# A two-layer hybrid encoder: wide products with weights stationary and 256 tokens streamed, residual stream kept by channels

## The chip, the cores and the metric

The kernel runs on one core of one Trainium2 chip. The metric is the device time of one execution in microseconds (us). A core has a matrix engine (PE, with PEld its weight loads), a vector engine (DVE), a scalar engine (ACT), a general engine (POOL) and a queue engine (SP) that here issues nearly all DMAs. Each engine takes its instructions in a fixed order and waits on semaphores for the others.

A matrix product holds one operand of 128x128 in the array (the stationary one, brought in by a load) and streams the other past it, column by column. Both operands have the contraction on their partitions; the result goes to PSUM with the stationary operand's columns on its partitions.

## The reference

```python
for i in range(DEPTH):                       # 2 layers, x is 256 tokens x 1024 channels, float32
    h = rms_norm(x, ffn1_norm[i])
    x = x + 0.5 * swiglu_ffn(h, ffn1_w_gate[i], ffn1_w_up[i], ffn1_w_down[i])   # 1024 -> 2816 -> 1024
    h = rms_norm(x, mix_norm[i])
    (s5_u, gla_q, gla_k, gla_v, gla_g, gla_zf, gla_zb, at_q, at_k, at_v) = split(h @ w_in[i])
    y_s5, y_gla, y_attn = s5_branch(...), gla_branch(...), attn_branch(...)     # each 256 x 512
    gates = sigmoid(h @ w_merge_gate[i] + b_merge_gate[i])                      # 3 x 1024 columns
    merged = sum(gates[b] * (y[b] @ w_branch[b]) for b in range(3))
    x = x + merged @ w_out[i]
    h = rms_norm(x, ffn2_norm[i])
    x = x + 0.5 * swiglu_ffn(h, ffn2_w_gate[i], ffn2_w_up[i], ffn2_w_down[i])
return rms_norm(x, final_norm)
```

## The kernel before

**Wide products.** Every large product is made of three products of float32r operands: `load` brings a weight tile (two 128-row k tiles by 512 columns) by DMA, ACT rounds it to `hi` (L209) and DVE makes the rest `lo` (L210); activations are split the same way (`hTh`/`hTl`, `sTh`/`sTl`, `mTh`/`mTl`, the branches' `y..h`/`y..l`). `mm3` (L219 to L221) then does hi.hi, hi.lo and lo.hi. The stationary operand is a 128x128 tile of activations, channels on partitions, 128 tokens as columns; 512 columns of weights are streamed, so the result has tokens on partitions. There are two token tiles (`NT` = 2).

**Where transposes come from.** The residual `x` is held with tokens on partitions. `norm` transposes it on PE (L263, four 128x128 transposes into one PSUM tile `pt`, four such tiles), multiplies by the gain (L265), splits it (L267, L268), and gets the sum of squares from ACT's accumulator (L272); the root `rstd` goes into the evacuations as one number per partition. In `ffn`, `evac` takes a block of 256 gate and 256 up columns: ACT does silu from PSUM (L294), DVE the product (L295), PE transposes the result twice (L298), ACT and DVE split it (L300, L301). GLA's q and k are transposed in `ev_tr` (L714), the gated sum in `merge` (L1127).

**One product in the other form.** `s5_glu` (L887 to L889) has weights stationary already and streams 256 tokens: `hi[:, ms]` is the stationary operand and `yh[:, k]` the moving one.

**Order.** `stream` goes over blocks of 512 columns in chunks of four k tiles; its first two blocks take their chunks in turn (`lead=2`). `weave` emits a main part and, after each of its steps, some steps of side parts: the S5 tables of a layer (`s5_tables`) beside the FFNs ahead of the mixer, the three branches inside the mixer. A scheduler then sets each engine's order from what was emitted. The tables end, for each quarter, in products `kp` on PE (L603), copies `ks` (L606, L607, L610), POOL copies `kx` (L627) and eight DMAs to DRAM (L630).

Of the kernel before, what the change touches and what calls it, by code (L numbers as in the profile page):

```python
# [15 lines left out]
P = 128  # L16
D = 1024
# [21 lines left out]
# main steps before a side part begins, and its steps per main step  # L39
# [12 lines left out]
# columns of the constants: those for the mixer, then those for the tables  # L52
# [4 lines left out]
def constants():  # L57
    """Arrays that depend on shapes alone, one row per partition."""
# [24 lines left out]
def cols(*parts):  # L83
    """Columns of weights [K, N] side by side: for the k tiles [a, z)."""
    def f(a, z):
        res, o = [], 0
        for w, cs in parts:
            res.append((w[a * P:z * P, cs].rearrange("(k p) n -> p k n", p=P), 0, o))
            o += cs.stop - cs.start
        return res  # L90
    return f


def weave(main, sides, up=nullcontext):
    """Emit main; from its step `start` on, `per` steps of a side part after each step of main.
    sides: list of [start, per, generator]. Whatever is left of them comes in the end."""
# [14 lines left out]
def rest(*gens):  # L111
    """Emit what is left of these parts, in turn, as one step."""
# [13 lines left out]
class Enc:  # L126
    def __init__(self, tc, ctx, ins, out):
# [15 lines left out]
        self.x = c.tile([P, NT, D], F32, name="x")  # L143
        self.cst = c.tile([P, C_MIX], F32, name="cst")
        self.row = {}
        with tc.high_priority():
            self.vectors("ffn1_norm", eng=nc.scalar)
            for h in range(2):
                for t in range(NT):
                    hs = slice(h * 512, (h + 1) * 512)  # L150
                    nc.scalar.dma_start(self.x[:, t, hs], ins["x"][0, t * P:(t + 1) * P, hs])
# [13 lines left out]
    def vectors(self, *names, eng=None):  # L165
        """Parameters of channels, to partitions: [128 channels, (layer, tile)]"""
        nc = self.nc
        eng = eng or nc.sync
        n = 48 if len(names) > 1 else 16
# [3 lines left out]
        for name in names:  # L173
# [6 lines left out]
            else:  # L180
                eng.dma_start(vec[r:r + DEPTH * KD], self.ins[name].rearrange("l (k p) -> (l k) p", p=P))
                self.row[name] = (vt, r, KD)
# [10 lines left out]
    def load(self, pieces):  # L193
        """pieces: list of (dram AP [partitions, k tiles, columns], first partition, first column)"""
# [21 lines left out]
    def mm3(self, ps, act, w, first, last):  # L216
        """act: (hi, lo) [128 k, 128 tok]; w: (hi, lo) [128 k, n]"""
# [4 lines left out]

    def stream(self, act, nk, blocks, lead=1):
        """act(k, t) -> (hi, lo). blocks: list of (pieces(k0, k1) in k tiles, width, evac(t, ps)).
        The first `lead` blocks take their first chunks together."""
# [3 lines left out]
        ps = {}  # L229
        for b, c in order:  # L230
            pieces, width, evac = blocks[b]
            k0, k1 = chunks[c]
            w = self.load(pieces(k0, k1))
            for t in range(NT):
# [6 lines left out]
            for s in range(0, k1 - k0, SUB):  # L241
                for t in range(NT):
                    for k in range(k0 + s, min(k1, k0 + s + SUB)):
                        self.mm3(ps[b, t][:, :width], act(k, t), w[k - k0], k == 0, k == nk - 1)
            if c == len(chunks) - 1:
                for t in range(NT):
                    evac(t, ps[b, t][:, :width])
            yield

# [1 line left out]
    def norm(self, name, l):  # L251
# [3 lines left out]
        sq = self.st.tile([P, 2, NT], F32, name=f"sq{self.n}", tag="sq")  # L255
# [3 lines left out]
        for c in range(2):  # L259
            for t in range(NT):  # L260
                pt = self.ptr.tile([P, 4, P], F32, name=self.nm("pt"), tag="tr")
# [915 lines left out]
```

## Time and profile before

| | |
|---|---|
| median of three runs | 1378.12 us (1378.01 to 1379.51) |
| profiled execution, span | 1376.2 us |
| PE busy | 1336.0 us, 97% |
| PE weight loads busy | 1061.6 us, 77% |
| DVE busy | 1018.4 us, 74% |
| ACT busy | 698.6 us, 51% |
| DMA queue of the weights, share of 16 engines | 57.5% |
| granted TensorE clock, mean | 0.996 |

The span is that of one profiled execution, from its first to its last instruction; 1.9 us lie between it and the median. Busy times of matrix products overlap, because products are pipelined: the pitch from start to start is what counts, and it is read from the timeline.

### The profile page before, as it was taken

How to read it: one execution, taken by the hardware profiler on the slowest of the kernel's cores; microseconds unless marked ns; L12 is line 12 of the kernel's file. 1: busy time of each engine (PE TensorE's matmuls, PEld its weight loads, DVE VectorE, ACT ScalarE, POOL GpSimd, SP SyncE). 2: the span in 40 equal slices, each digit the busy share in tenths (PEclk: the TensorE clock that was granted, in tenths of full speed). 3: DMA queues.
4: the chain of work that ended last, by engine and by line, in shares of the span. 5: the costliest groups of instructions: out<-in, count | busy, mean ns of one | idle time of the engine just before them, and what ended most of it. 6: DMA issues, size and time to landing. Idle time of an engine off the chain costs nothing.

```text
span 1376.2 us, 19506 instructions
## 1 busy us (share of the span) xinstructions
PE 1336.0 (97%) x6920; PEld 1061.6 (77%) x6920; DVE 1018.4 (74%) x1826; ACT 698.6 (51%) x1102; POOL 73.5 (5%) x104
## 2 busy tenths in 40 slices
PE   7999999999999999999999999999999999999997
PEld 5878788778787678768877777887787877888886
DVE  5899975779986789996465775457799767655553
ACT  5545345447585355445355454354475754555542
POOL 1020210000100000110000000000001000000000
PEclk9999999999999999999999999999999999999999
DMA  7766666565453366666665646566654533655662
GB/s 227 195 211 224 234 222 179 189 205 198 140 183 122 107 161 206 200 202 221 198 195 173 204 149 204 180 178 202 196 200 134 168 107 122 191 178 186 182 213 76
DMA packets 201201, 249.88 MB, mean 182 GB/s; under 512 B 40856, under 2 KB 134600, under 8 KB 201104
## 3 DMA queue, kind: packets, MB, share of 16 engines
q1 hardware_dynamic: 200496, 247.59, 57.5%
q8 instruction: 54, 0.88, 0.3%
q10 hardware_dynamic: 608, 1.06, 0.2%
q14 instruction: 43, 0.35, 0.1%
HBM read 234.44 MB, written 13.11 MB: 180 GB/s over the span
## 4 chain that ended last, share of the span: by engine, by line
PE 63%; issue 17%; DVE 13%; DMA 3%; ACT 3%; POOL 1%; SPq 0%; POOLq 0%; ACTq 0%; DVEq 0%
PE mm L220 18%; PE mm L219 17%; PE mm L221 17%; DVE lo L210 4%; PE S L818 1%; DMA raw<-in_ffn_w_gate 1%; DMA raw<-in_ffn_w_up 1%; PE as L1070 1%; ACT hi L209 1%; PE ao L1092 1%; DVE t L349 1%; PE st L298 1%; DVE run L836 1%; DVE run L835 1%; PE apt L1085 1%
## 5 line engine op out<-in xcount | busy, mean ns | idle before, releaser
L210 DVE TENSOR_TENSOR lo<-raw,hi 128x1024 fp32r<-128x1024 f32 x412 | 499.4, 1217 | 191.7 <-ACT hi L209 184.1
L209 ACT CAST hi<-raw 128x1024 fp32r<-128x1024 f32 x412 | 427.7, 1042 | 305.6 <-PE mm L221 276.3
L220 PE MATMUL mm<-lo,hTh 128*128 128x512 f32 (+1 forms) x1120 | 445.3, 398 | 5.3 <-DVE lo L210 4.9
L219 PE MATMUL mm<-hi,hTh 128*128 128x512 f32 (+1 forms) x1120 | 437.6, 396 | 2.7 <-ACT hTh L267 2.7
L221 PE MATMUL mm<-hi,hTl 128*128 128x512 f32 (+1 forms) x1120 | 436.1, 392 | 0.0
L220 PEld LDWEIGHTS mm<-lo,hTh 128*128 128x128 f32 x1120 | 211.2, 189 | 51.7 <-DVE lo L210 9.2
L219 PEld LDWEIGHTS mm<-hi,hTh 128*128 128x128 f32 x1120 | 211.2, 189 | 45.5 <-ACT hTh L267 3.8
L221 PEld LDWEIGHTS mm<-hi,hTl 128*128 128x128 f32 x1120 | 210.6, 188 | 40.6 <-DVE hTl L268 0.3
L220 PE MATMUL mm<-lo,sThffn 128*128 128x512 f32 x352 | 138.9, 395 | 2.0 <-DVE lo L210 2.0
L221 PE MATMUL mm<-hi,sTlffn 128*128 128x512 f32 x352 | 138.1, 393 | 0.0
L219 PE MATMUL mm<-hi,sThffn 128*128 128x512 f32 x352 | 136.4, 395 | 0.0
L300 ACT CAST sThffn<-st 128x256 fp32r<-128x256 f32 x88 | 32.6, 372 | 128.7 <-PE st L298 128.5
L220 PEld LDWEIGHTS mm<-lo,sThffn 128*128 128x128 f32 x352 | 66.4, 189 | 16.6 <-DVE lo L210 2.5
L221 PEld LDWEIGHTS mm<-hi,sTlffn 128*128 128x128 f32 x352 | 66.5, 189 | 14.1
L219 PEld LDWEIGHTS mm<-hi,sThffn 128*128 128x128 f32 x352 | 66.5, 189 | 13.8
L301 DVE TENSOR_TENSOR sTlffn<-st,sThffn 128x256 fp32r<-128x256 f32 x88 | 36.9, 421 | 50.3 <-ACT sThffn L300 49.9
L294 ACT ACTIVATE t<-mm,rstd 128x256 f32<-128x256 f32 x88 | 41.6, 475 | 43.0 <-PE mm L221 40.2
L295 DVE SCALAR_TENSOR_TENSOR t<-mm,rstd,t 128x256 f32<-128x256 f32 x88 | 41.4, 479 | 12.6 <-ACT t L294 12.4
L818 PEld LDWEIGHTS S<-U,bb 64*128 64x128 f32 x256 | 24.6, 187 | 12.8 <-issue 11.2
L298 PE MATMUL st<-ident,t 128*128 128x128 f32 x176 | 33.4, 272 | 0.0
L298 PEld LDWEIGHTS st<-ident,t 128*128 128x128 f32 x176 | 24.4, 140 | 11.3
L349 DVE TENSOR_TENSOR t<-e,S 128x256 f32<-128x256 f32 x64 | 22.4, 414 | 12.7 <-DMA e<-scr 6.9
(355 smaller groups left out, 1452.6 us busy)
## 6 DMA issues: line engine op xcount, KB each, us to landing
raw<-in_ffn_w_gate SPq DMA_DIRECT2D x176, 256.0 KB, 3.7
raw<-in_ffn_w_up SPq DMA_DIRECT2D x176, 256.0 KB, 4.4
raw<-in_ffn_w_down SPq DMA_DIRECT2D x88, 512.0 KB, 4.6
raw<-in_w_in SPq DMA_DIRECT2D x48, 512.0 KB, 4.4
raw<-in_w_merge_gate SPq DMA_DIRECT2D x48, 512.0 KB, 3.8
raw<-in_w_out SPq DMA_DIRECT2D x16, 512.0 KB, 4.6
scr<-e SPq DMA_DIRECT2D x6, 768.0 KB, 3.7
e<-scr SPq DMA_DIRECT2D x6, 768.0 KB, 5.7
```

The costliest lines, as they stand in the source:

```text
L209: nc.scalar.copy(hi[:, :e - s, :width], raw[:, :e - s, :width])
L210: nc.vector.tensor_tensor(lo[:, :e - s, :width], raw[:, :e - s, :width], hi[:, :e - s, :width].bitcast(F32), op=ALU.subtract)
L219: nc.tensor.matmul(ps, act[0], w[0], start=first, stop=False)
L220: nc.tensor.matmul(ps, act[0], w[1], start=False, stop=False)
L221: nc.tensor.matmul(ps, act[1], w[0], start=False, stop=last)
L294: nc.scalar.activation(sg, ps[:, :256], AF.Silu, scale=rstd[:, t:t + 1])
L295: nc.vector.scalar_tensor_tensor(s, ps[:, 256:], rstd[:, t:t + 1], sg, op0=ALU.mult, op1=ALU.mult)
L298: nc.tensor.transpose(pt[:, j], s[:, j * P:(j + 1) * P], self.ident)
L300: nc.scalar.copy(h, pt)
L301: nc.vector.tensor_tensor(sl[:, 2 * b:2 * b + 2, t * P:(t + 1) * P], pt, h.bitcast(F32), op=ALU.subtract)
L349: self.nc.vector.tensor_tensor(out, a, b, op=ALU.mult)
L818: nc.tensor.matmul(S[g][:, r, a * 64:(a + 1) * 64], bb[rows, a, r], U[rows, pair[a]], start=True, stop=True)
```

## The change

The residual is kept as `xT`, channels on partitions, all 256 tokens as columns. `x` arrives with tokens on partitions and is transposed once, in the first norm (`to_channels`); it is transposed back (`to_tokens`) beside the last FFN, whose down product keeps the old form, as do five of the seven blocks of `w_in`. All other wide products take `mm3T`: a 128x128 tile of weights is stationary, and 256 tokens are streamed; one PSUM tile holds two such results (a pair). The norm makes its squares by channels, adds them on POOL (L313, L314), sums over partitions by a product with ones (`pm`, L317), and spreads the root over all partitions by a second one (`pr`, L325), so that evacuations multiply by a row of 256 roots (`by_root`). The bias of the gates goes into ACT's tanh, and its twelve broadcast DMAs go.

```diff
     def mm3(self, ps, act, w, first, last):
...
+    def mm3T(self, ps, act, w, first, last, after=None):
+        nc = self.nc
+        m = nc.tensor.matmul(ps, w[0], act[0], start=first and after is None, stop=False, skip_group_check=True)
...
+        nc.tensor.matmul(ps, w[0], act[1], start=False, stop=False, skip_group_check=True)
+        nc.tensor.matmul(ps, w[1], act[0], start=False, stop=last, skip_group_check=True)
+        return m
...
             for s in range(0, k1 - k0, SUB):
+                ks = range(k0 + s, min(k1, k0 + s + SUB))
+                if not pairs:
+                    for t in range(NT):
+                        for k in ks:
+                            self.mm3(ps[b, t][:, :width], act(k, t), w[k - k0], k == 0, k == nk - 1)
+                    continue
+                for j, pair in enumerate(pairs):
+                    for i, n in enumerate(pair):
+                        for k in ks:
+                            wk = [x[:, n * P:(n + 1) * P] for x in w[k - k0]]
+                            m = self.mm3T(ps[b, j][:, i * SEQ:(i + 1) * SEQ], act(k), wk, k == 0, k == nk - 1,
+                                          cleared[b, j] if k == 0 and i else None)
...
-                for k in range(4):
-                    nc.tensor.transpose(pt[:, k], self.x[:, t, (4 * c + k) * P:(4 * c + k + 1) * P], self.ident)
-                f = self.t2([P, 4, P])
-                nc.vector.tensor_tensor(f, pt, g[:, 4 * c:4 * c + 4].unsqueeze(2).to_broadcast((P, 4, P)), op=ALU.mult)
...
+        for j, src in self.to_channels() if first else ((j, self.xT[:, 2 * j:2 * j + 2]) for j in range(KD // 2)):
+            for i in range(2):
+                k = 2 * j + i
+                nc.scalar.activation(hi[:, k], src[:, i], AF.Copy, scale=g[:, k:k + 1])
+                nc.vector.scalar_tensor_tensor(lo[:, k], src[:, i], g[:, k:k + 1], hi[:, k].bitcast(F32),
+                                               op0=ALU.mult, op1=ALU.subtract)
...
+        for j in range(KD // 2):
+            s = self.t2([P, 2, SEQ]) if j else sums
+            nc.scalar.activation(s, self.xT[:, 2 * j:2 * j + 2], AF.Square)
+            if j:
+                nc.gpsimd.tensor_tensor(sums, sums, s, op=ALU.add)
+        nc.gpsimd.tensor_tensor(sums[:, 0], sums[:, 0], sums[:, 1], op=ALU.add)
...
+            nc.tensor.matmul(pm[:, t], sums[:, 0, t * P:(t + 1) * P], self.ones[:, :2], start=True, stop=True)
...
+            nc.vector.tensor_scalar(dg[:, t], self.ident, rstd[:, t:t + 1], None, op0=ALU.mult)
...
+        nc.tensor.matmul(pr, self.ones, dg.rearrange("p t i -> p (t i)"), start=True, stop=True)
...
+        nc.scalar.copy(self.root, pr)
...
+    def by_root(self, out, ps):
+        self.mul(out, ps, self.root.unsqueeze(1).to_broadcast((P, 2, SEQ)))
...
-                    nc.scalar.activation(sg, ps[:, :256], AF.Silu, scale=rstd[:, t:t + 1])
-                    nc.vector.scalar_tensor_tensor(s, ps[:, 256:], rstd[:, t:t + 1], sg, op0=ALU.mult, op1=ALU.mult)
...
-                        nc.tensor.transpose(pt[:, j], s[:, j * P:(j + 1) * P], self.ident)
...
+                    gu = self.t2([P, 2, SEQ])
+                    self.by_root(gu, ps)
+                    nc.scalar.activation(gu[:, 0], gu[:, 0], AF.Silu)
+                    self.mul(gu[:, 0], gu[:, 0], gu[:, 1])
+                    h = sh[:, 2 * b + j]
+                    nc.scalar.copy(h, gu[:, 0])
+                    nc.vector.tensor_tensor(sl[:, 2 * b + j], gu[:, 0], h.bitcast(F32), op=ALU.subtract)
...
+                return lambda j, ps: self.by_root(dst[:, 2 * j:2 * j + 2], ps)
...
-                for k in range(4):
-                    nc.tensor.transpose(pt[:, k], gates[0][:, t, (4 * c + k) * P:(4 * c + k + 1) * P], self.ident)
...
+            self.split_into(mh[:, ks], ml[:, ks], gates[0][:, ks])
```

The first place is PE in the first FFN of layer 0, where a block of gate and up columns has ended and the next runs. `mm` are the PSUM tiles of the blocks, `st` that of the transposes; L298 is the transpose in `evac`, L444 (before) and L529 (after) a transpose of the tables. Before:

```order
L219 MATMUL mm_225<-hi_367,hTh_119 128x512
L220 MATMUL mm_225<-lo_368,hTh_119 128x512
L298 MATMUL st_293<-ident,t_290 128x128 x2
L221 MATMUL mm_225<-hi_367,hTl_120 128x512
L220 MATMUL mm_226<-lo_368,hTh_119 128x512
L221 MATMUL mm_226<-hi_367,hTl_120 128x512
```

After:

```order
L232 MATMUL mm_269<-hTl_122,hi_455 128x256
L233 MATMUL mm_269<-hTh_121,lo_456 128x256
L529 MATMUL lmT<-ident,lm 128x32 x3
L227 MATMUL mm_576<-hTh_121,hi_565 128x256
L232 MATMUL mm_576<-hTl_122,hi_565 128x256
L233 MATMUL mm_576<-hTh_121,lo_566 128x256
```

The pairs of transposes are gone from between the wide products, which are now of 256 columns and twice as many.

The second place is PE at the start of layer 0's mixer. Before, the last products of the FFN's down part, the norm's transposes `pt` and the mixer's first products:

```order
L220 MATMUL mm_2116<-lo_2339,sThffn_169 128x512
L221 MATMUL mm_2116<-hi_2338,sTlffn_170 128x512
L263 MATMUL pt_2365<-ident,x 128x128 x4
L263 MATMUL pt_2374<-ident,x 128x128 x4
L263 MATMUL pt_2383<-ident,x 128x128 x4
L219 MATMUL mm_2433<-hi_2423,hTh_2363 128x512
L220 MATMUL mm_2433<-lo_2424,hTh_2363 128x512
```

After, the end of the mixer's two lead blocks (`mm_3214` is the last tile of the second), the norm's two small products and the third block:

```order
L219 MATMUL mm_3214<-hi_3287,hTh_3110 128x288
L220 MATMUL mm_3214<-lo_3288,hTh_3110 128x288
L221 MATMUL mm_3214<-hi_3287,hTl_3111 128x288
L317 MATMUL pm_3140<-ones,t_3128 128x2 x2
L325 MATMUL pr_3149<-dg_3146,ones 128x256
L227 MATMUL mm_3381<-hTh_3110,hi_3371 128x256
L232 MATMUL mm_3381<-hTl_3111,hi_3371 128x256
```

The transposes ahead of the mixer's first product are gone; `pm` and `pr` stand with nothing between them, behind both lead blocks and ahead of the third.

The third place is POOL at the same point of the program: `kx` are the copies of the last quarter of the tables, `rstd` the root. Before:

```order
L617 TENSOR_TENSOR e_2013<-r_418,tcst 128x512
L627 COPY kx_1963<-ks_1913 128x2x64 x4
L627 COPY kx_2214<-ks_2167 128x2x64 x4
L277 TENSOR_TENSOR rstd_2361<-ms_2409,mhalf 128x2
L907 MEMSET t_3095 128x384
```

After:

```order
L705 TENSOR_TENSOR e_2593<-r_524,tcst 128x512
L715 COPY kx_2878<-ks_2807 128x2x64 x4
L986 MEMSET t_3903 128x384
L987 MEMSET t_3903 128x4x2
L313 TENSOR_TENSOR t_3128<-t_3128,t_3130 128x512
L313 TENSOR_TENSOR t_3128<-t_3128,t_3133 128x512
L313 TENSOR_TENSOR t_3128<-t_3128,t_3136 128x512
L314 TENSOR_TENSOR t_3128<-t_3128 128x256
L320 TENSOR_TENSOR rstd_3109<-ms_3143,mhalf 128x2
```

Three additions of 128x512 and one of 128x256 now stand between the last `kx` and the root. On PE the products `kp` that the last `kx` waits for stood some 90 products ahead of the mixer's first one; now they stand among the lead blocks, and 60 wide products (24 of 512 columns, 36 of 288) follow them ahead of `pm`.

## Rows read from the trace of the kernel before

**Rows 1.** The page, part 1: busy time, share of the span, instructions.

```profile
PE 1336.0 (97%) x6920; PEld 1061.6 (77%) x6920; DVE 1018.4 (74%) x1826; ACT 698.6 (51%) x1102; POOL 73.5 (5%) x104
```

**Rows 2.** Timeline of PE, FFN down product: start us, us, engine, line.

```profile
200.04 0.39 PE L219 MATMUL mm<-hi,sThffn 128*128 128x512 f32 x1
...
205.94 0.39 PE L221 MATMUL mm<-hi,sTlffn 128*128 128x512 f32 x1
```

**Rows 3.** Timeline of PE in `s5_glu`; last, its loads: ns min/median/max.

```profile
411.09 0.28 PE L888 MATMUL glu<-ysl,hi 128*128 128x256 f32 x1
...
411.66 0.28 PE L887 MATMUL glu<-ysh,hi 128*128 128x256 f32 x1
...
412.56 0.28 PE L889 MATMUL glu<-ysh,lo 128*128 128x256 f32 x1
...
413.26 0.28 PE L889 MATMUL glu<-ysh,lo 128*128 128x256 f32 x1
...
L888 PEld LDWEIGHTS glu<-ysl,hi x32: 187/188/192, 407.7 to 1100.3; 128*128 128x128 f32 x32
```

**Rows 4.** Timeline of PE, last FFN: a pair of transposes among wide products.

```profile
1310.67 0.39 PE L221 MATMUL mm<-hi,sTlffn 128*128 128x512 f32 x1
1310.90 0.38 PE L298 MATMUL st<-ident,t 128*128 128x128 f32 x2
...
1311.58 0.39 PE L221 MATMUL mm<-hi,sTlffn 128*128 128x512 f32 x1
```

**Rows 5.** Stretches of PE at four norms, last a merge: length, PE busy, clock.

```profile
216.14:222.07 5.93, 5.42 (x31) 1.00 0.67 185
495.63:505.80 10.17, 6.86 (x31) 0.83 0.62 133
698.70:703.80 5.10, 3.97 (x25) 1.00 0.44 131
...
1178.70:1184.30 5.60, 5.00 (x29) 1.00 0.57 177
469.90:483.40 13.50, 12.12 (x60) 1.00 0.43 133
```

**Rows 6.** Groups by line and shape: busy us, mean ns, idle before.

```profile
L295 DVE SCALAR_TENSOR_TENSOR t<-mm,rstd,t 128x256 f32<-128x256 f32 x88 | 41.4, 479 | 12.6 <-ACT t L294 12.4
L301 DVE TENSOR_TENSOR sTlffn<-st,sThffn 128x256 fp32r<-128x256 f32 x88 | 36.9, 421 | 50.3 <-ACT sThffn L300 49.9
L298 PE MATMUL st<-ident,t 128*128 128x128 f32 x176 | 33.4, 272 | 0.0
L265 DVE TENSOR_TENSOR t<-pt,vecT 128x512 f32<-128x512 f32 x24 | 16.0, 681 | 2.8 <-PE pt L263 2.8
L355 DVE TENSOR_TENSOR la<-t 128x256 f32<-128x256 f32 x16 | 6.5, 413 | 0.0
```

**Rows 7.** Stretches, tables beside FFNs: length; PE, PEld, DVE, ACT, POOL busy.

```profile
120.00:180.00 60.00, 57.96 (x345) 45.93 (x344) 60.00 (x98) 27.14 (x39) 13.93 (x11) 0.97 0.71 238
...
530.00:590.00 60.00, 59.65 (x311) 47.51 (x310) 58.82 (x203) 29.83 (x44) 8.25 (x17) 1.00 0.63 199
```

**Rows 8.** Timelines of POOL and its DMAs; then lines, min/median/max.

```profile
141.71 3.33 POOL L627 COPY kx<-ks 128x128 f32<-128x128 f32 x4 [23.47 <-DVE ks L610]
...
197.54 1.01 POOL L627 COPY kx<-ks 128x128 f32<-128x128 f32 x4 [18.77 <-DVE ks L610]
198.58 3.61 SPq L630 DMA_DIRECT2D scr<-kx  x8
...
DMA to landing us min/median/max: 1.5/1.6/3.3
...
L617 POOL TENSOR_TENSOR e<-r,tcst x8: 1342/1873/3492, 70.6 to 622.7; 128x512 f32<-128x512 f32 x8
...
L277 POOL TENSOR_TENSOR rstd<-ms,mhalf x6: 697/698/1642, 20.8 to 1187.0; 128x2 f32<-128x2 f32 x6
```

**Rows 9.** Timeline of PE, attention scores: plain float32 products of 256 columns.

```profile
1100.85 1.13 PE L1070 MATMUL as<-akT,aqT 64*128 64x256 f32 x4
```

More of the change, by code (lines that the diff above doesn't have):

```diff
@@ L228, in stream @@
         order += [(b, c) for b in range(lead, len(blocks)) for c in range(len(chunks))]
-        ps = {}
+        ps, cleared = {}, {}
         for b, c in order:
-            pieces, width, evac = blocks[b]
+            pieces, width, evac, *pairs = blocks[b]
+            pairs = pairs[0] if pairs else None
             k0, k1 = chunks[c]
             w = self.load(pieces(k0, k1))
-            for t in range(NT):
+            for t in range(len(pairs) if pairs else NT):
                 if c == 0:
@@ new lines, in norm @@
+        sums = self.t2([P, 2, SEQ])
+        for j in range(KD // 2):
+            s = self.t2([P, 2, SEQ]) if j else sums
[3 more added lines that the diff above has]
+        nc.gpsimd.tensor_tensor(sums[:, 0], sums[:, 0], sums[:, 1], op=ALU.add)
+        pm = self.ptr.tile([P, NT, 2], F32, name=self.nm("pm"), tag="tr")
+        for t in range(NT):
+            nc.tensor.matmul(pm[:, t], sums[:, 0, t * P:(t + 1) * P], self.ones[:, :2], start=True, stop=True)
@@ L281, in ffn @@
-    def ffn(self, l, which):
+        dg = self.st.tile([P, NT, P], F32, name=self.nm("dg"), tag="dg", bufs=1)
+        for t in range(NT):
+            nc.vector.tensor_scalar(dg[:, t], self.ident, rstd[:, t:t + 1], None, op0=ALU.mult)
+        pr = self.ptr.tile([P, SEQ], F32, name=self.nm("pr"), tag="tr")
+        nc.tensor.matmul(pr, self.ones, dg.rearrange("p t i -> p (t i)"), start=True, stop=True)
+        self.root = self.st.tile([P, SEQ], F32, name=self.nm("root"), tag="root", bufs=1)
@@ L282, in ffn @@
+    def ffn(self, l, which, first=False, last=False):
         nc, ins = self.nc, self.ins
@@ L307, in ffn @@
                 cs = slice(b * 256, (b + 1) * 256)
-                blocks.append((cols((wg, cs), (wu, cs)), 512, evac(b)))
+                blocks.append((cols((wg, cs), (wu, cs)), 512, evac(b), ((0, 2), (1, 3))))
             yield from self.stream(act, KD, blocks, lead=2)
+            sact = self.parts(sh, sl)
+            if not last:
+                yield from self.stream(sact, KF, [(cols((wd, slice(c * 512, (c + 1) * 512))), 512, self.add_half(c),
+                                                   ((0, 1), (2, 3))) for c in range(2)])
+                return
             def down(c):
@@ L1146, in run @@
         self.mixer(1)
-        weave(self.ffn(1, "ffn2"), [])
-        self.final()
+        with self.tc.tile_pool(name="xout", bufs=1) as xp:
+            self.x = xp.tile([P, NT, D], F32, name="x")
+            weave(self.ffn(1, "ffn2", last=True), [[4, 1, self.to_tokens()]])
+            self.final()
 def tile_encoder(tc, ins, out):
```

174 lines of the change are left out of this document (89 added, 85 removed).

## The prediction

> **What bounds the kernel now.** I read the page's busy shares first: PE 97%, DVE 74%, ACT 51% [rows 1]. A PE that is busy can still be slow, so the timeline of PE comes next, in a stretch where nothing but wide products runs: from 200.04 to 205.94 us there are 26 steps, 0.2269 us from one product of 512 columns to the next [rows 2]. The kernel has 4800 such products and 96 of 288 columns. At 0.227 and 0.128 us they are 1102 of the 1376 us. So PE sets the time, and what is not wide product on PE (some 274 us: small products, transposes, waits) is where a change can gain. Third, I read what each break in the wide stream costs (rows 4 and 5), and fourth the stretches in which DVE too is full [rows 7], because there a change that gives DVE work moves the end.
>
> **The wide products in the new form.** 4152 of the 4800 products become 8304 products of 256 columns; the columns streamed are the same, the loads of the stationary operand double. The trace has this very form in `s5_glu`: 256 tokens past weights. In its better stretch, 411.09 to 411.66 us, five steps take 0.57 us, 0.114 each (0.1134 is exactly half of the pitch in rows 2); in its worse one, 412.56 to 413.26, six steps take 0.70, 0.117 each [rows 3]. So the doubled loads are hidden under 256 columns, and the whole question is which of the two paces holds. Against 0.1134 the worse one costs 8304 x 0.0036 = 30 us, the better nothing (rounded rows; with a last digit the other way it is up to 5 us below nothing to 35 above). I take 0.1144, a cost of 8 us, nearer the better pace: that is the one in the stretch without breaks around it, and the long FFN stretches have still fewer, while the worse stretch stands between breaks.
>
> The Trainium skill's page "TensorE: Matmul & The Clock Gate", section "Part 3: Packing small matmuls" (what overlaps and what doesn't), says that a weight load runs beside a running product only when the two use different row groups; all wide products use all rows, so each load would add its own time. Rows 3 speak against it: a load lasts 188 ns there and the products still follow each other every 0.114 us.
>
> **What goes from PE.** (1) In the FFNs 88 pairs of transposes. From 1310.67 to 1311.58 us there are three wide products and one pair: 0.91 less 0.68 is 0.23 us [rows 4]; 88 x 0.23 = 20.2. (2) Five norms lose their transposes and PE's waits for DVE between them. The stretches last 5.93, 10.17, 5.10 and 5.60 us [rows 5], and the wide products that start in them (14, four of them narrow; 11; 9; 12) are worth 2.78, 2.50, 2.04 and 2.72: lost are 3.15, 7.67, 3.06 and 2.88; the fifth norm, ahead of layer 1's mixer, I take like the third. Together 19.8. (3) Each merge: 13.50 us for 42 products worth 9.53, so 3.97 [rows 5], twice 7.9. (4) GLA's q and k: four groups of eight transposes. A further transpose after the first takes 0.11 (0.38 for two in rows 4 against 0.27 for one in rows 6), so 0.23 + 6 x 0.11 = 0.9 a group, 3.6 in all. Sum: 51.5 us go.
>
> **What comes on PE.** (5) `to_tokens`: four groups of four transposes, 0.23 + 2 x 0.11 = 0.45 each: 1.8. (6) `pm` and `pr` in six norms. They are plain float32, which the trace carries out as two passes each: four passes of 256 columns take 1.13 us [rows 9], 0.25 for each further one, so `pr` is 0.5; `pm` is four loads and next to no columns, 0.11 each like a transpose, 0.45; with the breaks that both make, 1.2 us. Six times: 7.2.
>
> **Waits at the new norm.** The root now goes through ACT's squares, four POOL additions, PE, DVE, POOL, DVE and PE again, in place of ACT, DVE, POOL. In the FFN norms some 22 us of lead blocks cover it. (7) At the start of layer 0's mixer it is not covered. `pm` stands behind the lead blocks, the third block needs PSUM that only an evacuation with the root frees, and POOL has the tables' last `kx` in front, whose products on PE now stand 60 wide products (24 x 0.227 + 36 x 0.128, 10 us) ahead of `pm`. The squares use memory that is free only when `kx` is in DRAM. After those products: `kx` and its eight DMA issues, 4.65 us when DVE left POOL alone (197.54 to 202.19), the landing 1.6, two squares at about 0.7 (a 128x512 operation in rows 6), three additions at 1.34 to 1.87 and half a one, then `pm` and the root with 0.45, 0.70 and an evacuation of 0.7 [rows 6, 8]: 14.2 to 16.1, less 10, is 4 to 6, and with up to 3 of waiting in DVE's and ACT's queues 4 to 9. I take 7, and 1 for the clock: after the long wait at 500 us the granted clock of the stretch was 0.83 [rows 5], so part of it ran at the lower level of 1.2 GHz. Queued behind the waiting `pm` are all wide products; behind the squares on ACT the next roundings. (8) The two norms behind a merge must wait for the merge's own operand tile before they split, as in rows 5 now (10.17 and 5.60): I take 3 and 2 us, most of it waiting at `pm` for POOL, bounds 1 and 4 each. The two other norms and the two merges at 0.6 each: 2.4. Together 15.4.
>
> **DVE.** An FFN evacuation now has a 128x512 operation from PSUM and two of 128x256: 0.68 + 0.41 + 0.41 = 1.50, against 0.48 + 0.42 = 0.90 [rows 6]. That is 0.6 x 88 = 53 us more. Most of it lies beside PE work, but DVE is full at 60.00 of 60 us and 58.8 of 60 where the tables run [rows 7]. One FFN there has 22 evacuations, 13 us. (9) Bounds: nothing, if later stretches take up the tables (they do slip into the mixer, see 7), and 27 us if two FFNs pay in full. I take 5, near the lower end: with DVE full, PE is still busy 57.96 and 59.65 of 60 us there, and the down parts that follow have no evacuations of this kind, so the tables can slip there. What is late then is `lo`, and PE waits for it.
>
> The Trainium skill's "SBUF — State Buffer", section "SBUF: two separate sides", says that POOL and DVE share a port pair by an exclusive lock, which a DVE operation with two SBUF inputs needs too. The trace agrees: the same four `kx` took 1.01 us at 197.5 and 3.33 at 141.7, where DVE was full [rows 7, 8]. Held by the rule, the new additions would take some 5 us from DVE in each of the two norms beside tables, 5 us more than my sum; without it, none.
>
> **The sum.** -51.5 + 1.8 + 7.2 + 15.4 + 8 + 5 = -14.1 us, from 1376.2 to 1362.1 of span; with the 1.9 us between span and median, 1364.
>
> **Rivals.**
> - The worse pace everywhere, 0.117: 30 in place of 8, 1386, slower. For it speaks that half of the steps of rows 3 are of that kind; against it the rows just before, which stay at 0.114 once reached. From 0.1161 us a product on, the sum changes sign.
> - DVE becomes the bound beside the tables: 27 in place of 5, again 1386. For it rows 7; against it that the same operations may slip behind.
> - All covers hold: the better pace and no new wait for DVE, -13, so 1351. For it that rows 2 keep one pitch over the whole stretch.
> - Loads exposed: 4152 more loads at 0.108 us (a transpose's pitch, rows 4 and 6), 448 us more, 1804 with the better pace. Rows 3 exclude it nearly. It is what the overlap rule of the Trainium skill's TensorE page would give.
> - That the change doesn't do what it says can be set aside: the order of PE shows 8304 products of 256 columns and the `st`, `qkT` and `mT` transposes gone.
>
> **How the numbers follow.** Forecast 1364: 0.56. Better pace and covers, 1351: 0.17. Worse pace, 1386: 0.17. DVE bound, 1386: 0.09. Loads exposed: 0.01. A measurement of this kernel tells about 0.2%, 3 us, from no change. Faster by more: 0.17 and 0.50 of the forecast, 0.67. Same: 0.05 of the forecast and 0.03 of the DVE case, 0.08. Slower: the rest, 0.25. The range: below, the better pace with the mixer's wait at 4 and small waits behind the merges, 1340; above, the worse pace with 6 us of the other waits, 1392; beyond lie both rivals at once and a wait of 9.
>
> **What would show it.** In the profile after: a pitch of 0.113 to 0.115 us in the FFN's down stretch (else the pace failed); no transposes between FFN products, with PE's instructions near 10,800; one wait of PE of 4 to 9 us ahead of `pm` of layer 0's mixer, released by POOL; waits of wide products for `lo` not over some 10 us in all; DVE busy about 1065 us. It would be wrong if the pitch is 0.117 or more in long stretches, if PE waits for `lo` by tens of us, or if the wait at the mixer is far over 9.

## The result

The changed kernel takes 1401.61 us (median of four runs, 1399.16 to 1403.01), the kernel before 1378.45 beside it: a ratio of 1.017, 95% interval 1.0156 to 1.0185. It is slower by 23 us, where 1364 was forecast. The profiled execution has a span of 1401.1 us.

### The profile page after: what moved, and what is told of

Its sections match the earlier page's. It is cut to its first block, busy times and chain, and to the rows that moved or that the text cites. A ratio compares the mean times of both kernels' runs of the same rounds, so it can differ in the third digit from the quotient of the medians.

```text
span 1401.1 us, 27541 instructions
## 1 busy us (share of the span) xinstructions
PE 1354.9 (97%) x10804; PEld 1278.3 (91%) x10804; DVE 1071.4 (76%) x1934; ACT 695.0 (50%) x1120; POOL 138.6 (10%) x129
## 4 chain that ended last, share of the span: by engine, by line
PE 76%; issue 15%; DVE 3%; DMA 2%; POOL 1%; ACT 1%; SPq 1%; ACTq 0%; POOLq 0%; DVEq 0%
PE mm L233 20%; PE mm L232 20%; PE mm L227 20%; PE mm L220 2%; PE mm L219 2%; PE mm L221 2%; PE S L897 2%; DVE lo L210 1%; PE as L1149 1%; PE ao L1171 1%; POOL kx L715 1%; PE yp L935 1%; DMA raw<-in_ffn_w_up 1%; DMA raw<-in_w_in 1%; PE apt L1164 1%
## 5 line engine op out<-in xcount | busy, mean ns | idle before, releaser
L210 DVE TENSOR_TENSOR lo<-raw,hi 128x1024 fp32r<-128x1024 f32 x412 | 499.1, 1214 | 227.2 <-ACT hi L209 218.0
L232 PE MATMUL mm<-hTl,hi 128*128 128x256 f32 x1920 | 550.5, 288 | 2.5 <-DVE hTl L303 2.5
L227 PE MATMUL mm<-hTh,hi 128*128 128x256 f32 x1920 | 547.5, 288 | 5.3 <-ACT hTh L302 4.3
L233 PE MATMUL mm<-hTh,lo 128*128 128x256 f32 x1920 | 548.4, 288 | 0.6 <-DVE lo L210 0.5
L227 PEld LDWEIGHTS mm<-hTh,hi 128*128 128x128 f32 x1920 | 371.7, 195 | 7.7 <-ACT hTh L302 5.1
L232 PEld LDWEIGHTS mm<-hTl,hi 128*128 128x128 f32 x1920 | 373.4, 194 | 5.0 <-DVE hTl L303 3.4
L233 PEld LDWEIGHTS mm<-hTh,lo 128*128 128x128 f32 x1920 | 372.1, 195 | 2.9 <-DVE lo L210 1.0
L219 PE MATMUL mm<-hi,hTh 128*128 128x512 f32 (+1 forms) x160 | 60.6, 386 | 9.4 <-ACT hi L209 9.4
L715 POOL COPY kx<-ks 128x128 f32<-128x128 f32 x32 | 44.5, 1430 | 204.4 <-DVE ks L698 179.2
L220 PE MATMUL mm<-lo,hTh 128*128 128x512 f32 (+1 forms) x160 | 61.6, 385 | 0.0
L221 PE MATMUL mm<-hi,hTl 128*128 128x512 f32 (+1 forms) x160 | 60.4, 382 | 0.0
L219 PEld LDWEIGHTS mm<-hi,hTh 128*128 128x128 f32 x160 | 30.4, 191 | 14.9 <-ACT hi L209 9.6
```

The costliest lines, as they stand in the source:

```text
L210: nc.vector.tensor_tensor(lo[:, :e - s, :width], raw[:, :e - s, :width], hi[:, :e - s, :width].bitcast(F32), op=ALU.subtract)
L219: nc.tensor.matmul(ps, act[0], w[0], start=first, stop=False)
L220: nc.tensor.matmul(ps, act[0], w[1], start=False, stop=False)
L221: nc.tensor.matmul(ps, act[1], w[0], start=False, stop=last)
L227: m = nc.tensor.matmul(ps, w[0], act[0], start=first and after is None, stop=False, skip_group_check=True)
L232: nc.tensor.matmul(ps, w[0], act[1], start=False, stop=False, skip_group_check=True)
```

## The profile after

The page, part 1, of the changed kernel (answers to [rows 1]):

```profile
PE 1354.9 (97%) x10804; PEld 1278.3 (91%) x10804; DVE 1071.4 (76%) x1934; ACT 695.0 (50%) x1120; POOL 138.6 (10%) x129
```

PE has 10804 instructions and DVE 1071 us of work, both near the forecast. POOL has 139 us in place of 73.5, more than its new additions explain: the larger ones, 18 of 128x512, are 27.8 us, while `kx` alone went from 18.3 to 44.5. Now the pitch. Timeline of PE in the changed kernel, FFN down products (answers to [rows 2]), and further down the products of a branch, where y streams; columns: start us, us, engine, line:

```profile
195.65 0.28 PE L227 MATMUL mm<-sThffn,hi 128*128 128x256 f32 x1
...
196.85 0.28 PE L232 MATMUL mm<-sTlffn,hi 128*128 128x256 f32 x1
...
482.12 0.28 PE L227 MATMUL mm<-yah,hi 128*128 128x256 f32 x1
...
484.05 0.28 PE L233 MATMUL mm<-yah,lo 128*128 128x256 f32 x1
```

From 195.65 to 196.85 us lie ten steps, 0.120 each. From 482.12 to 484.05 lie 17, 0.1135 each. The two differ in the tile that streams, and in nothing else that the program shows: same helper, same weight tiles, same size. Over the whole trace the products with hT, sT and mT (7728 of them) follow each other at 0.120, those with y (576 in the branches, 96 in `s5_glu`) at 0.113 to 0.118.

The stages, in windows that run from the first wide product of a stage to that of the next. Of the kernel before layer 0's first FFN and the two mixers, then of the changed kernel the same and layer 0's second FFN; columns: stretch, length, then busy us (instructions) of PE, PEld, DVE, ACT, POOL, then the granted clock, DMA share, GB/s:

```profile
11.60:218.60 207.00, 203.95 (x1093) 163.61 (x1093) 185.34 (x441) 102.34 (x146) 27.21 (x38) 0.99 0.70 213
218.60:419.00 200.40, 197.57 (x1159) 156.30 (x1159) 163.08 (x257) 117.75 (x210) 9.49 (x8) 1.00 0.57 179
...
901.90:1102.00 200.10, 196.84 (x1158) 155.91 (x1155) 162.67 (x257) 117.36 (x210) 8.02 (x7) 1.00 0.56 179
```

```profile
9.90:227.20 217.30, 207.10 (x1804) 203.99 (x1805) 195.80 (x467) 102.19 (x147) 40.62 (x38) 0.98 0.66 203
227.20:442.70 215.50, 207.45 (x1562) 184.44 (x1560) 169.53 (x267) 118.78 (x216) 18.32 (x17) 0.95 0.54 164
...
519.50:726.10 206.60, 199.80 (x1657) 197.75 (x1658) 176.69 (x413) 93.18 (x131) 31.80 (x28) 0.98 0.63 191
...
922.80:1123.90 201.10, 199.94 (x1531) 179.05 (x1529) 167.15 (x262) 116.57 (x214) 16.04 (x11) 0.99 0.57 173
```

The very first product of layer 0's mixer in the changed kernel was scheduled ahead, to 218.29 us, among the last ones of the FFN; its window begins with the second, at 227.2, so the wait ahead of the first counts to the FFN. The lengths side by side, with two of the experiments below (windows of each trace by the same rule; "branches" begin with the first product of a branch and hold the merge):

| stage | before | after | e5 | e8 |
|---|---|---|---|---|
| FFN 1, layer 0 | 207.0 | 217.3 | 211.8 | 200.5 |
| mixer, layer 0 | 200.4 | 215.5 | 214.4 | 221.2 |
| branches, layer 0 | 81.9 | 76.8 | 77.1 | 77.0 |
| FFN 2, layer 0 | 200.7 | 206.6 | 199.8 | 192.9 |
| FFN 1, layer 1 | 200.3 | 196.7 | 188.2 | 187.4 |
| mixer, layer 1 | 200.1 | 201.1 | 201.6 | 204.2 |
| branches, layer 1 | 79.6 | 76.8 | 76.0 | 77.0 |
| FFN 2, layer 1 | 185.8 | 191.8 | 184.7 | 184.6 |

The branches gain 3 to 5 us each (transposes of the merge gone). The last FFN, which has no tables beside it and no long wait, is 6 us longer; in e5, where only the place of tiles differs, it takes 184.7. The two stages with most of the loss are layer 0's first FFN and mixer, 10 and 15 us. What stands at their border, first on PE, then POOL, then SP's queue (columns: start us, us, engine, line, and in brackets the idle time before it and what ended it):

```profile
218.29 0.80 PE L219 MATMUL mm<-hi,hTh 128*128 128x512 f32 x1 [9.40 <-ACT hi L209]
218.88 0.42 PE L233 MATMUL mm<-sThffn,lo 128*128 128x256 f32 x1
219.09 0.42 PE L227 MATMUL mm<-sThffn,hi 128*128 128x256 f32 x1
...
251.92 1.01 PE L317 MATMUL pm<-ones,t 128*128 128x2 f32 x4 [6.49 <-POOL t L314]
254.50 1.22 PE L325 MATMUL pr<-dg,ones 128*128 128x256 f32 x2 [1.56 <-DVE dg L323]
```

```profile
193.31 14.71 POOL L715 COPY kx<-ks 128x128 f32<-128x128 f32 x4 [3.63 <-DVE ks L698]
207.98 1.04 POOL L705 TENSOR_TENSOR e<-r,tcst 128x512 f32<-128x512 f32 x1
```

```profile
208.04 3.78 SPq L718 DMA_DIRECT2D scr<-kx  x8
211.92 0.39 SPq L206 DMA_DIRECT2D raw<-in_ffn_w_down  x1
212.41 3.15 SPq L206 DMA_DIRECT2D raw<-in_w_in  x6
```

Read from the bottom: SP issues no weights until 208, because the eight stores of `kx` stand ahead of them in its queue; the stores wait for POOL, whose four copies take 14.71 us where the same four took 1.01 in [rows 8]. In those 14.7 us DVE is busy for 13.85, and from 200 to 208 us the DMA share is 0.01. PE runs dry at 208.9. The Trainium skill's page "SBUF — State Buffer", section "SBUF: two separate sides", says that POOL and a DVE operation with two SBUF inputs hold a port pair of the on-chip memory exclusively, for a whole instruction. The trace agrees that POOL is held out, at 14.71 us for 1.01, and here it lasts over a row of some twenty DVE instructions. It is not always POOL that waits: at 188.26 us an `e` on POOL took 1.41 us beside a busy DVE, and there the DVE instruction beside it, an `hTl`, took 1.26 us where the next of its kind took 0.47.

Last, the clock. Windows of the changed kernel in which it was granted the lower level of 1.2 GHz (the first three of eight ahead of the end, and the sum of the eight), then, of the kernel before, the sum of its two:

```profile
212.50:222.70 10.20, 4.41 (x19) 4.32 (x20) 5.77 (x8) 3.13 (x3) 0.00 (x0) 0.50 0.93 321
250.10:260.30 10.20, 6.82 (x29) 6.55 (x30) 0.87 (x4) 3.31 (x11) 2.40 (x3) 0.50 0.57 120
284.20:291.00 6.80, 6.80 (x26) 5.66 (x25) 2.70 (x5) 1.04 (x1) 0.00 (x0) 0.50 0.81 267
...
sum 47.60, PE 36.44 PEld 34.01 DVE 29.43 ACT 17.26 POOL 9.47; mean PE 4.55 PEld 4.25 DVE 3.68 ACT 2.16 POOL 1.18
```

```profile
sum 6.80, PE 6.80 PEld 5.36 DVE 6.80 ACT 2.29 POOL 0.00; mean PE 3.40 PEld 2.68 DVE 3.40 ACT 1.14 POOL 0.00
```

PE works for 36.4 us at that level, 6.8 before. A product takes 0.21 us there (218.88 to 219.09) in place of 0.120, so some 16 us of it are lost, and of the 6.8 before at most half: an estimate of 12 to 13 us more than before. The first two windows begin within PE's two long waits; the third stands in a stretch where PE is busy throughout, and why the clock fell there is not settled.

## The experiments

**e1: streams alone.** The loop of the kernel, called for each pair of places:

```
for i in range(count):
    m0 = mo // 4 + (i % ks) * 512
    s0 = so // 4 + (i % kw) * 128
    o = 256 * (i % 2) if two else 0
    nc.tensor.matmul(ps[:, o:o + cols], st[:, s0:s0 + 128], mv[:, m0:m0 + cols], start=i == 0, stop=i == count - 1,
                     skip_group_check=True)
```

> This kernel leaves the encoder out: it holds nothing but streams of 48 products (one stationary load and one product each, as in the changed kernel) on the same x, so that each stream's pitch can be read by itself. The start of the stationary slice is moved by 0, 32, 64, 128 and 192 bytes against a 128-byte line, that of the moving slice by 0 to 512 bytes; behind these stand streams of 512, 384, 320, 288, 192 and 128 columns, streams with zeros as data, and streams that keep one moving or one stationary slice. Theory A (relative place): in the changed kernel all moving tiles with 0.120 us and all weight tiles begin 64 bytes past a 128-byte line, while the y tiles with 0.113 to 0.118 begin on the line; so 256 columns give 0.120 where both starts are alike modulo 128 and 0.113 to 0.118 where they differ. Theory B (absolute place): 0.120 wherever the moving slice begins at 64 past a line, 0.113 to 0.118 where it begins on the line, whatever the stationary slice does. Theory C (no place, a constant of the form): 0.120 in all of them, 512 columns 0.2267, with some 0.0133 us a product beside the columns. Theory D (data): zeros give another pitch than x.

Timeline of PE in this kernel. A row is a stream of 48 products; its pitch is the next row's start less its own, by 48 (the last row of a group only closes the one before it). Both tiles begin at 128 modulo 256; the names give the bytes by which the stationary and then the moving slice are shifted from there (zero, thirty: 32, sixty: 64, ninety: 96, hund: 128, ninetytwo: 192; q: other numbers of columns, e 512, d 384, a 192, s 128; zboth: zeros as data). "Ahead" is the lower address:

```profile
140.36 5.60 PE L43 MATMUL psixtyxzero<-rb,wb 128*128 128x256 f32 x48
145.80 5.84 PE L43 MATMUL psixtyxthirty<-rb,wb 128*128 128x256 f32 x48
151.47 5.92 PE L43 MATMUL psixtyxsixty<-rb,wb 128*128 128x256 f32 x48
157.22 5.82 PE L43 MATMUL psixtyxninety<-rb,wb 128*128 128x256 f32 x48
...
196.47 5.62 PE L43 MATMUL phundxsixty<-rb,wb 128*128 128x256 f32 x48
201.93 5.84 PE L43 MATMUL phundxninety<-rb,wb 128*128 128x256 f32 x48
207.61 5.92 PE L43 MATMUL phundxhund<-rb,wb 128*128 128x256 f32 x48
213.36 5.82 PE L43 MATMUL phundxninetytwo<-rb,wb 128*128 128x256 f32 x48
...
275.91 11.09 PE L43 MATMUL qezeroxzero<-rb,wb 128*128 128x512 f32 x48
286.84 11.17 PE L43 MATMUL qezeroxsixty<-rb,wb 128*128 128x512 f32 x48
297.85 11.35 PE L43 MATMUL qesixtyxzero<-rb,wb 128*128 128x512 f32 x48
309.04 11.06 PE L43 MATMUL qesixtyxsixty<-rb,wb 128*128 128x512 f32 x48
319.94 8.51 PE L43 MATMUL qdzeroxzero<-rb,wb 128*128 128x384 f32 x48
...
423.02 5.52 PE L43 MATMUL qasixtyxsixty<-rb,wb 128*128 128x192 f32 x48
428.38 5.49 PE L43 MATMUL qszeroxzero<-rb,wb 128*128 128x128 f32 x48
433.71 5.53 PE L43 MATMUL qszeroxsixty<-rb,wb 128*128 128x128 f32 x48
...
461.34 5.92 PE L43 MATMUL zboth<-zb 128*128 128x256 f32 x48
467.10 5.92 PE L43 MATMUL onemov<-rb,wb 128*128 128x256 f32 x48
```

Both slices at the same place: 0.120 (151.47 to 157.22, and 207.61 to 213.36). The moving slice 64 bytes ahead: 0.1133 (140.36 to 145.80) and 0.1137 (196.47 to 201.93). The slice 32 behind that (145.80 to 151.47): 0.1181. Of all 40 pairs, the seven alike modulo 256 gave 0.1196 to 0.1200, five with the moving slice 64 bytes ahead modulo 256 gave 0.1133 to 0.1140, a sixth of that kind (192 and 128) 0.1178, and the rest 0.1174 to 0.1197. So of theory A the relative place holds, but not as it was written: what counts is modulo 256, not 128 (the pairs 128 bytes apart gave 0.1185 to 0.1187, not 0.120), three pairs with the moving slice 96 behind gave 0.1197, hardly less than the same place, and one pair is an exception. B falls (moving slice at 64: 0.1179, 0.120, 0.1137 or 0.1187 by the stationary one), C and D fall (zeros: 0.120, as x at the same place). With 512 columns it is the other way round: the same place is best, 0.2277 and 0.2271, and 64 bytes ahead is worst, 0.2331. 192 and 128 columns take the same, 0.111 to 0.112, the nearest that a load and a product came in these streams.

**e2 and e3: 64 unused bytes**, in e2 between the weight tiles and all behind them, in e3 ahead of the weight tiles:

```diff
+        self.pad = pool("pad", 1).tile([P, 16], F32, name="pad")
+        nc.gpsimd.memset(self.pad, 0.0)
         self.hp = pool("hp", 1)
```

These are the lines of e2; in e3 the two stand ahead of `self.wraw`.

> The changed kernel with 64 unused bytes a partition between the weight tiles and all tiles behind them: the moving tiles hT, sT and mT begin on a 128-byte line (before: 64 past it), the y tiles 64 past it, the weights stay 64 past it. Theories A and B: hT, sT and mT fall from 0.120 to about 0.1165, some 7600 products by 0.0035 = 27 us less, 1375 us; the y products rise to 0.120. Theory C: no change, 1401 us and 0.120.

> The changed kernel with 64 unused bytes a partition ahead of the weight tiles, so that weights and moving tiles both shift: weights, hT, sT and mT begin on a 128-byte line, the y tiles 64 past it. Theory A (relative place): hT, sT and mT stay at 0.120, 1401 us. Theory B (absolute place): they fall to 0.1165 as in the run beside it, 1375 us. Theory C: 1401 us.

e2: 1391.94 us (1.0079 of before, 1.0062 to 1.0096), hT, sT and mT at 0.1177, y up to 0.1195. e3: 1401.74 us, hT, sT and mT at 0.120, y at 0.115 to 0.117. So between these two the difference of the places counts, and not the place. The gain of e2 is 10 us, not 27: its pitch fell by 0.0023, not 0.0035, 18 us for 7728 products, and not all of that reached the end.

**e5: 192 unused bytes** in the place of e2's 64 (`[P, 48]`). The weights lie at 192 modulo 256, hT, sT and mT then at 128.

> The changed kernel with 192 unused bytes a partition between the weight tiles and all tiles behind them: hT, sT and mT then begin 64 bytes ahead of the weights' place, counted modulo 256; the weights stay where they were. Theory A as the streams showed it (256 columns take 0.1133 where the moving slice lies 64 bytes ahead of a stationary slice that itself starts at 192, 0.118 at 64 behind, 0.120 at the same place): hT, sT and mT fall to between 0.1133 and 0.117, so some 7600 products give 23 to 50 us back; y, now 128 bytes off, goes to 0.1186. From 1401: 1351 to 1378. Theory A': only whether the places differ counts, and the pitch stays at 0.118 as with 64 bytes: 1390.

1375.80 us, 0.9976 of before (0.9962 to 0.999). Timeline of PE, an FFN down part of e5, and a wait; last, POOL:

```profile
173.87 0.28 PE L229 MATMUL mm<-sThffn,hi 128*128 128x256 f32 x1
...
175.91 0.28 PE L229 MATMUL mm<-sThffn,hi 128*128 128x256 f32 x1
...
203.15 0.58 PE L235 MATMUL mm<-sThffn,lo 128*128 128x256 f32 x1 [4.96 <-DVE lo L212]
```

```profile
166.48 18.02 POOL L717 COPY kx<-ks 128x128 f32<-128x128 f32 x4 [24.50 <-DMA scr<-cc]
```

18 steps in 2.04 us, 0.1133; over the whole trace 0.1144, which is what the prediction took. Two paces remain at this place: of the steps up to 200 us, beside the tables, about half are at 0.117 to 0.118, from 1200 to 1300 us, in the last FFN, nearly all at 0.113 to 0.114. What else sets them apart no run shows. Moving the tiles, the only edit, is worth 26 us of 1401.6. On paper 7728 x 0.0055 is 42. By the table the last FFN and layer 1's first give all of it back (7.1 and 8.5 us for 1056 and 1584 products); the mixers, with 768 such products each, give 1.1 and nothing; beside the tables the wait of 9.40 us is gone, but PE waits 4.96 us for `lo` at 198 us. It looks like the same chain, one quarter of the tables earlier: POOL's copies are held for 18.02 us, SP issues no weights from 169.0 to 188.2 us, and then an `e` on DVE, ahead of that `lo`, waits 4.55 us for a store of `e` to land. There other engines set the time once PE is quicker.

**e4: `kx` on ACT; e6: the stores on POOL's queue; e8: e5 with `kx` on ACT and `e` on DVE.**

```diff
-                nc.gpsimd.tensor_copy(kx[:, :, s], ks.rearrange("p g j f -> p g (j f)")[:, :, (3 - s) * 16:(3 - s) * 16 + 64])
+                nc.scalar.copy(kx[:, :, s], ks.rearrange("p g j f -> p g (j f)")[:, :, (3 - s) * 16:(3 - s) * 16 + 64])
```

That is e4's, and half of e8's; the other half of e8 turns the one `nc.gpsimd.tensor_tensor(ld["e"]` of the tables into `nc.vector.tensor_tensor(ld["e"]`. In e6 and e7:

```diff
-                    nc.sync.dma_start(scr[:, a:z], ld[name])
+                    nc.gpsimd.dma_start(scr[:, a:z], ld[name])
```

and the same for the store of `kx`.

> The changed kernel with the sixteen-fold copies kx of the tables on ACT instead of POOL. My theory: PE's wait of 9.57 us at 208.6 us comes from one group of four kx copies that takes 14.7 us on POOL while DVE is full; its eight DMA issues on SP stand ahead of the weights of the mixer, so no weights are loaded. On ACT the copies take under 1 us each, the wait goes to under 1 us, and the low clock right behind it goes too (about 10 us at half the pace, 5 us): 1401 less 12 to 17, 1384 to 1389 us. Rival (the weights wait for free tiles or for transfers): the wait stays within 2 us of 9.57, and the time within 3 us of 1401.

1403.41 us (1400.99 to 1405.36): no gain. The copies are quick now (0.90 us for four) and the weights come in time, but the next work on POOL is held in their place. POOL, SP, DVE and PE of e4:

```profile
200.96 17.82 POOL L705 TENSOR_TENSOR e<-r,tcst 128x512 f32<-128x512 f32 x1 [10.06 <-DMA scr<-e]
```

```profile
218.81 0.34 SPq L712 DMA_DIRECT2D scr<-e  x1
```

```profile
223.20 0.69 DVE L454 TENSOR_TENSOR e<-U,U 128x512 f32<-128x512 f32 x1 [5.32 <-DMA scr<-e]
223.81 0.68 DVE L345 SCALAR_TENSOR_TENSOR xT<-mm,xT 128x512 f32<-128x512 f32 x1
```

```profile
224.55 0.79 PE L219 MATMUL mm<-hi,hTh 128*128 128x512 f32 x1 [5.08 <-DVE xT L345]
```

DVE holds POOL for 17.8 us, and then waits itself for what POOL was late with: its next `e` needs the tile that the store empties, and the residual `xT` stands behind it in DVE's queue. So my theory had the place right and the cure wrong: it is not `kx` that is slow but whatever POOL has beside a full DVE. The mixer began 10 us earlier than in the changed kernel and lasted 5 us longer; the rest went behind it.

> The changed kernel with the tables' stores to DRAM (kx, bb, cc, e) issued from POOL's own queue in place of SP's, nothing else. My theory: both long waits of PE at layer 0's mixer come from the order on SP: at 208.6 us (9.57) the weights stand behind stores that wait for POOL, which DVE keeps from its memory (a copy group of 14.7 us); at 245 us (6.65) the squares wait for the kx stores, which stand behind nine weight loads on SP. Freed, the first goes under 2 us, the second to 2 to 4, and the low clock behind the first with them: 1401 less 12 to 20, 1381 to 1389. Rival (POOL itself is late, whichever queue its stores take, because DVE is full): the wait ahead of the mixer's first product goes, but the one ahead of pm grows by as much, and the time stays within 4 us of 1401.

1411.39 us, 10 more: the theory falls as well. Line views of e6 (count: duration ns min/median/max):

```profile
L712 POOL DMA_DIRECT2D scr<-bb x6: 557/592/780, 125.9 to 824.5; - x6
...
L718 POOL DMA_DIRECT2D scr<-kx x64: 512/512/557, 141.2 to 899.9; - x64
```

A store costs POOL 0.5 to 0.6 us, 82 of them some 44, on the engine that was late already; PE no longer waits ahead of the mixer's first product, but it waits 4.46 for `lo` in the FFN's end, 0.91 for `xT` in the mixer's lead blocks, and at `pm` 7.85 in place of 6.49. The stores had stood only 1.4 us behind the weights at `pm` (POOL was done with `kx` at 237.29, SP began at 238.74), so there was little to gain there. The Trainium skill's "SBUF — State Buffer", section "SBUF: two separate sides", warns of it: descriptors of such DMAs are made by POOL, which DVE can lock out. The trace agrees as far as it goes: from issue to landing the `kx` stores take up to 6.2 us here, 3.3 in [rows 8].

> Both edits of the two runs beside it. If pace and waits are separate causes, the gains add within 4 us: about 1335 to 1366. If the faster products only lay more on DVE and the weight loads, less: over 1366.

1390.56 us: 21 less than e6. The pace gives 21 where it gave 26 in e5, and the queue costs 15 on top of e5's time where it cost 10. The two edits added would give 1385.6; the 5 us beyond are just over what the expectation allowed for separate causes, so that they are separate is not shown. This edit is a loss with either pace.

> The changed kernel with 192 unused bytes as in the run beside it, and the tables' work on POOL taken off it: kx on ACT and the small products e on DVE (four of 128x512, 0.7 us each per layer); the stores stay on SP's queue. My theory (POOL starved beside a full DVE holds the stores and with them the weights): the wait ahead of the mixer's first product goes under 2 us, that ahead of pm keeps 4 to 7 (the stores still stand behind weight loads), 8 to 15 us less than with the 192 bytes alone. Rival (it is transfers or free tiles that are late): no more than 3 us less.

1363.65 us (1362.48 to 1366.10), 0.9887 of before (0.9869 to 0.9905), 12 less than e5: as my theory had it. PE has no wait ahead of the mixer's first product and one of 0.97 us, for `xT`, in its lead blocks; POOL has 80 us of work. The wait at `pm` stays, 7.43 us. By the table the first FFN gives 11.3 us back and the next one, beside layer 1's tables, 6.9; the mixer between them takes 6.8, so 12 is what is left of more. This version beats both kernels.

**e9: y moved too; e10: the tables earlier; e11: squares in other memory.** All on e8:

```diff
+            ypad = mp.tile([P, 16], F32, name=f"ypad{l}")        # e9, e10, e11
...
-PREP = ((2, 1.8), (6, 0.85))
+PREP = ((0, 2.2), (6, 0.85))                                     # e10
...
-            s = self.t2([P, 2, SEQ]) if j else sums
+            s = sq[j]         # e11: halves of two "raw" weight tiles
```

> The run with 192 unused bytes and the tables' work off POOL (1363.65 us), and 64 unused bytes more a partition ahead of the mixer's own tiles, so that the y tiles too come to the place (128 modulo 256, the weights at 192) at which hT, sT and mT took 0.1144. Theory A (relative place): the y products (1536, now 0.1185 to 0.1193) fall to between 0.1133 and 0.116, 4 to 8 us less: 1356 to 1360. Rival (the pitch of y belongs to the stretches between breaks, not to the place): no change, 1362 to 1366, y at 0.118 to 0.119.

1363.75 us: no change. The pitch of y did fall, from 0.118 to 0.119 (in e5) to 0.115 to 0.117, as theory A has it, but the expectation counted 1536 products where there are 672: 2 us, which is less than the runs differ by.

> The run beside it with layer 0's tables begun with the first step of the first FFN, not the third, and 2.2 steps of them for each of the FFN's in place of 1.8. My theory: layer 0's mixer loses some 20 us against the kernel before, about 10 by two waits of PE at pm and pr (7.6 and 1.8), because the squares need the memory of the last kx, and about 10 more by the low clock behind them (10.2 us at 239 and 10.2 us at 273 us). With the tables done earlier the first wait falls to under 3 and the low clock at 239 with it: 6 to 14 us less than the run beside it. Rival (DVE is full up to there, so an earlier start only moves its queue, and lo comes late in the first FFN instead): within 3 us of the run beside it, the waits of PE for lo in the first FFN up by 4 or more.

1366.96 us: 3.2 more than e9, at the rival's bound of 3. Yet the first half of my theory holds: `pm` now waits for nothing, and layer 0's mixer lasts 207.6 us in place of 219.4. The first FFN takes 210.3 in place of 200.6, with 2.2 us of waiting for the tables and 2.24 for `lo` at its start. DVE's work only moves: 7 us more of it in the first FFN, 8 less in the mixer.

> The run with the y tiles moved, and the norm's four squares put into two of the five tiles that the raw weights pass through, in place of the memory that the tables leave. My theory (the squares wait for the last kx to reach DRAM): PE's wait at pm of layer 0's mixer falls from 7.6 to 1 to 4 us and less of the low clock follows: 5 to 12 us less than the run beside it without this. Rival (with two of five tiles gone the next weights come late, or the squares now wait for a weight tile): the wait at pm or at the products behind it stays over 6 us, and the time is within 3 us or longer.

1401.35 us, 38 more. The wait at `pm` of layer 0's mixer is gone, as my theory had it, but PE waits 5.81 us for `cc` from DVE just ahead of it, and in the time the rival holds, and more: the first product of the kernel waits 8.03 us for weights, and each FFN behind a merge 5.

**e12: e8's table edit in the kernel before.**

> The kernel before, with the tables' work taken off POOL as in the runs beside it (kx on ACT, e on DVE); a control. My theory: the 12 us that this gave in the changed kernel are a cost that the change brought (its DVE is fuller beside the tables, and POOL is held from memory): here it gives under 3 us, 1376 to 1381. Rival (the tables' work on POOL costs in both kernels): 6 us less or more, under 1373.

1376.43 us, 0.9979 of before (0.9969 to 0.9988): 3.2 us less, at the edge of what I expected. So, as an estimate, of e8's 12 us some 9 belong to what the change brought, 3 to both kernels. Against this version of before, e8 is 13 us faster.

## Why the prediction was wrong

- **The pace, the step that failed.** "I take 0.1144, a cost of 8 us" came from [rows 3], `s5_glu`; measured was 0.120, beyond even the rival of 0.117. The row was read rightly and carried over wrongly. In the kernel before y begins at byte 161472 of a partition and the weights at 48128, that is at 192 and 0 modulo 256, y 64 bytes ahead: the pair that gave 0.1137 in e1. In the changed kernel hT (81600) and the weights (48832) both lie at 192. What made the step look safe was that 0.1134 is half of 0.2269. In e1 512 and 256 columns at the same place take 0.227 and 0.120: 0.107 for 256 columns, and some 0.013 that every product pays once. At the same place 4152 more products pay it, some 55 us on paper. Undoing the place (e5) gave 26 us back.
- **What goes from PE.** The transposes went, the branches gained 3 to 5 us, PE's count is as forecast. With the pace that was assumed and POOL freed (e8) the FFNs of layer 1 are 12.9 and 1.2 us shorter than before; the first is more than the some 5 us that its terms give (22 pairs, a norm), the last within some 2 us of them.
- **Waits at the new norm.** "One wait of 4 to 9 us ahead of `pm`": 6.49, and 1.56 at `pr`. The mechanism is the one told: POOL's `kx` copies began at 235.74 us, SP issued their stores at 238.74 to 243.58, and the squares began at 245.03. "1 for the clock" was too small: 10.2 us at the lower level behind this wait alone, 6.8 of them busy. Layer 0's mixer is 14 us longer than layer 1's, where 8 were counted for wait and clock.
- **The wait that was not forecast**: 9.40 us ahead of the mixer's first product, from POOL held by DVE, through SP's queue, to the weights. The prediction weighed the port for the new additions and for `kx`, and asked of SP only what stands ahead of `pm`; that all weights stand behind the same stores it did not ask. e8 less e5 prices this chain, with the clock behind it and its like in layer 1's tables: 12 us. In e5 it showed as the 4.96 us for `lo`, so the 12 are its price at the quicker pace; at the pace of the changed kernel e4 and e6 only moved the wait.
- **DVE.** An FFN evacuation now has, in groups of the changed kernel by line and shape (busy us, mean ns):

```profile
L434 DVE TENSOR_TENSOR t<-mm,root 128x512 f32<-128x512 f32 x88 | 59.7, 683 | 1.4 <-PE mm L233 0.5
L372 DVE TENSOR_TENSOR sTlffn<-t,sThffn 128x256 fp32r<-128x256 f32 x88 | 35.7, 427 | 1.9
L434 DVE TENSOR_TENSOR t<-t 128x256 f32<-128x256 f32 x88 | 34.4, 415 | 0.9 <-ACT t L368 0.9
```

  0.68 + 0.43 + 0.42 = 1.53 us, 1.50 forecast. PE waits little for `lo` (2.3 us at 670); the fuller DVE was paid for by POOL, which e12 bears out: off POOL, the same work gains 12 us with the change and 3 without.
- **The sum.** 1401.6 less 25.8 (e5) and 12.1 (e8) is 1363.7, and the forecast was 1364. That it meets so well is chance. Put to the stages, the forecast's terms give the two mixers some 9 us more, the branches with the merge and the norm behind it 16 less, and the four FFNs 7 less (an estimate; a norm lies across a border). In e8 the mixers are 25 us longer than before, the branches 7 shorter and the FFNs 28 shorter. Why the mixers lost and the FFNs gained so much beyond the terms was not taken apart.
- **Loads exposed** is excluded, as the rows said: loads of 0.19 us each and products every 0.12. The overlap rule of the Trainium skill's page "TensorE: Matmul & The Clock Gate" ("Part 3: Packing small matmuls") does not describe this stream.

## What to carry to other kernels

A pitch that is read from one stretch holds for another only if operands lie alike: before carrying it over, compare where the stationary and the moving tile begin, and price the fixed part by product, not by column. A change that gives one engine (here DVE) more work can be paid for by another that it holds (POOL), and by whatever waits in a queue behind that one's results: ask of every such queue what else stands in it. Sixty-four or 192 unused bytes are a cheap experiment.

## What the runs showed of the hardware

- The pitch of float32r products of 128 rows and 256 columns, each with its own load, depends on where the two slices begin: 0.120 us at the same place modulo 256, 0.1133 to 0.1140 with the moving one 64 bytes ahead (one exception at 0.1178), 0.1174 to 0.1197 otherwise; for 512 columns 0.227, 0.2331 and 0.2294 (moving slice 64 behind). At the same place neither zeros as data nor a slice that stays the same changes it. Why is open: no run here shows the mechanism.
- POOL beside DVE: the same four small copies took 1.01 us ([rows 8], at 197.54) and, where DVE was full, 3.33 ([rows 8]), 14.71 and 18.02; one operation of 128x512 beside a busy DVE took 17.82 in e4 and 1.41 at 188.26 us of the changed kernel. What decides which of the two is held was not tried.
- Stores issued on POOL's own queue cost it 0.5 to 0.6 us each.
- Not tried, and so open: why the clock fell at 284 us, where PE was busy throughout.
